# A SwiGLU layer's gate and up products with seven block products for eight over half of K

## The chip, the cores and the metric

One NeuronCore of one Trainium2 chip runs the whole program. The metric is device time in microseconds (us), the median over runs of the same program. The engines are TensorE (PE in the profile; PEld is its weight load), VectorE (DVE), ScalarE (ACT), GpSimd (POOL) and SyncE (SP, which here only issues transfers); 16 DMA engines move data.

## What is computed

A decoder layer over 256 tokens with a width of 2048, in float32: a token mixer of three attention branches, and then a dense SwiGLU layer, with a norm before each and at the end. The change lies in the second part (`w_gate` and `w_up` are 2048x5632, `w_down` 5632x2048):

```python
def rms_norm(x, g):
    y = x * lax.rsqrt(jnp.mean(x * x, axis=-1, keepdims=True) + RMS_EPS)
    return y * g

def swiglu(h, w_gate, w_up, w_down):
    return (jax.nn.silu(h @ w_gate) * (h @ w_up)) @ w_down

    ...
    h = rms_norm(x, norm_mix_g[l])
    x = x + hybrid_mixer(h, w_in[l], ...)
    h = rms_norm(x, norm_ffn_g[l])
    x = x + swiglu(h, w_ffn_gate[l], w_ffn_up[l], w_ffn_down[l])
    return rms_norm(x, final_norm_g)
```

## The kernel before

**Products in three parts.** TensorE multiplies in fp32r, a rounded float32. To keep float32's accuracy every operand is split into a high part (rounded to fp32r by a ScalarE copy) and a low part (the rest, subtracted on VectorE), and each product of a 128x128 stationary tile with a 128x512 moving tile is made three times: high x high, high x low, low x high (L714 to L716). The stationary tile is a piece of the transposed activations, the moving tile a piece of a weight matrix.

**Jobs, pieces and halves.** The program is one list of jobs (L194 to L199): 30 of `w_in`, 12 of `w_branch`, 4 of `w_out`, for each of the 11 column blocks j one of `w_fg` and one of `w_fu` (L552 to L554), 4 of `w_fd`. A job makes 512 output columns for both token tiles (t = 0, 1), in two banks of PSUM (`acc0`, `acc1`, from a pool of four). Its weights come in pieces of 512 rows (`raw`, 128x4x512, 1 MB), which SP loads three ahead into three buffers (`load`, L618). A piece is used in two halves. For each half `split` (L634) rounds 128x1024 on ScalarE (L655) and subtracts on VectorE (L656), three halves ahead of the products, into one of four buffers each; then come 12 products, 3 for each of two rows of K and two token tiles.

**Side work.** Transposes, attention and the like are generators in a queue; `advance(1)` takes one step of it before each half's products (L730), and a wanted operand that is not there is forced (`quad`, L156).

**The order.** The schedule is written out by hand: each engine runs its instructions in the order in which the program issues them, and waits by semaphores for the other engines' results and for buffers.

**Around the change.** The four `w_out` jobs end in `evac_out` (L491), which transposes x, times the norm's weight, into the quads `h2` (high and low parts, 512 rows of K each). The gate job's banks go through ScalarE's Silu with the norm's row factor into `sg` (L540); the up job's banks are multiplied by it on VectorE (L548). The product f is transposed by TensorE in two later side steps (L203, four transposes each) and split by ScalarE and VectorE (L212, L213) into 11 pairs of quads in the slot pool, which the down jobs read. The row factor of `up` is applied in the down jobs' evacuation.

```python
def evac_fu(j):
    def f(pss):
        s = sg.pop(j)
        for t in range(2):
            nc.vector.tensor_tensor(s[:, t], pss[t], s[:, t], OP.mult)
        side.append(to_quad(("f", j), s))
    return f
```

Of the kernel before, what the change touches and what calls it, by code (L numbers as in the profile page):

```python
# [23 lines left out]
F32 = mybir.dt.float32  # L24
F32R = mybir.dt.float32r
# [26 lines left out]
def trunk(ctx, tc, xT, x, gmix, gffn, w_in, b_gate, lq1, lk1, lq2, lk2, subln, w_branch, w_out,  # L52
          w_fg, w_fu, w_fd, gfin, out):
    nc = tc.nc
    cst = ctx.enter_context(tc.tile_pool(name="cst", bufs=1))
    raws = ctx.enter_context(tc.tile_pool(name="raws", bufs=RAW_BUFS))
    spl = ctx.enter_context(tc.tile_pool(name="spl", bufs=SPLIT_BUFS))
    hpool = ctx.enter_context(tc.tile_pool(name="hpool", bufs=4))
    slots = ctx.enter_context(tc.tile_pool(name="slots", bufs=SLOTS))

    small = ctx.enter_context(tc.tile_pool(name="small", bufs=4))
    accp = ctx.enter_context(tc.tile_pool(name="accp", bufs=4, space=bass.MemoryType.PSUM))
    side_ps = ctx.enter_context(tc.tile_pool(name="side_ps", bufs=2, space=bass.MemoryType.PSUM))
# [1 line left out]

    def slot(shape, name, dt=F32):
        return slots.tile(shape, dt, tag="slot", name=name)

    def sm(shape, name):
        return small.tile(shape, F32, name=name)  # L70
# [93 lines left out]

    def new_both():

        t = hpool.tile([P, 4, 2, S], F32R, tag="hq", name="hq")
        return t[:, :, 0], t[:, :, 1], t


    xq = {}
# [7 lines left out]
    def split_x(k):  # L179
        q = k // 4  # L180
        if q not in h_q:
            h_q[q] = new_both()
        h, l = h_q[q][:2]
# [302 lines left out]
    def row_rstd(dst, ssq):  # L486
        tot = sm([P, 2], "tot")
        nc.vector.tensor_reduce(tot, ssq, axis=AX.X, op=OP.add)
        rstd(dst, tot, float(D))

    def evac_out(c):  # L491
        def f(pss):
            xc = x2[c]
            for t in range(2):
                nc.vector.tensor_tensor(xc[:, t], pss[t], xc[:, t], OP.add)

            def go():
                yield
                both = new_both()
                h, l = both[:2]  # L500
                for kp in range(2):
                    ps = tps()
                    transposes(ps, [xc[:, t, (2 * kp + i) * P:(2 * kp + i + 1) * P]
                                    for i in range(2) for t in range(2)])
                    for i in range(2):
                        k = 2 * kp + i
                        gk = gf[:, 4 * c + k:4 * c + k + 1]
                        pk = ps[:, i * S:(i + 1) * S]
                        nc.scalar.activation(h[:, k], pk, AF.Copy, scale=gk)
                        nc.vector.scalar_tensor_tensor(l[:, k], pk, gk, h[:, k].bitcast(F32),  # L510
                                                       op0=OP.mult, op1=OP.subtract)
                    if kp == 1:
                        quads["h2", c] = both
                    yield
                row_sums(ssq2, c, xc)
                if c == 3:
# [12 lines left out]
        job([(w_out[c, kp], ("m", kp)) for kp in range(4)], evac_out(c))  # L529


    sg = {}

    def evac_fg(j):
        def f(pss):
            quad("rs2")
            s = slot([P, 2, 512], "sg")
            sg[j] = s
            for t in range(2):
                nc.scalar.activation(s[:, t], pss[t], AF.Silu, scale=rs2[:, t:t + 1])  # L540
        return f

    def evac_fu(j):

        def f(pss):
            s = sg.pop(j)
            for t in range(2):
                nc.vector.tensor_tensor(s[:, t], pss[t], s[:, t], OP.mult)  # L548
            side.append(to_quad(("f", j), s))
        return f  # L550

    for j in range(NCF):  # L552
        job([(w_fg[j, kp], ("h2", kp)) for kp in range(4)], evac_fg(j))
        job([(w_fu[j, kp], ("h2", kp)) for kp in range(4)], evac_fu(j))  # L554


    ssq3 = cst.tile([P, 2, 5], F32, name="ssq3")
# [1 line left out]
    gfs = {}  # L559

    def load_gfin():
        g = hpool.tile([P, 4, 512], F32, tag="hq", name="gfin")
# [47 lines left out]
    down_job = len(jobs)  # L610
    for c in range(4):
        job([(w_fd[c, kp], ("f", kp)) for kp in range(NCF)], evac_down(c))


    pieces = [(ji, pi) for ji, (ps, _) in enumerate(jobs) for pi in range(len(ps))]
    raw = {}

    def load(pidx):  # L618
        if pidx >= len(pieces):
            return  # L620
        ji, pi = pieces[pidx]
        ap = jobs[ji][0][pi][0]
        t = raws.tile([P, 4, 512], F32, tag="raw", name="raw")
        raw[pidx] = t
        if pidx < 4:
            for a, n in ((0, 1), (1, 1), (2, 2)) if pidx == 0 else ((0, 2), (2, 2)):
                load_xT(4 * pidx + a, n)
                nc.sync.dma_start(t[:, a:a + n], ap[:, a:a + n])  # L628
        else:
            nc.sync.dma_start(t, ap)  # L630

    parts = {}

    def split(hidx):  # L634
        if hidx >= 2 * len(pieces):
            return
        pidx, hf = divmod(hidx, 2)
        if 0 < hidx < 8:
            for i in range(2):
                split_x(2 * hidx + i)  # L640
        r = raw[pidx][:, 2 * hf:2 * hf + 2]
        if hidx < 2 * len(pieces) - LAST + SPLIT_BUFS:
            h = spl.tile([P, 2, 512], F32R, tag="wh", name="wh")
            l = spl.tile([P, 2, 512], F32R, tag="wl", name="wl")
        else:
            both = hpool.tile([P, 2, 2, 512], F32R, tag="hq", name="wboth")
            h, l = both[:, 0], both[:, 1]
        if hidx < 2:
            for i in range(2):
                if hidx == 0:  # L650
                    split_x(i)
                nc.scalar.activation(h[:, i], r[:, i], AF.Copy)
                nc.vector.tensor_tensor(l[:, i], r[:, i], h[:, i].bitcast(F32), OP.subtract)  # L653
        else:
            nc.scalar.activation(h, r, AF.Copy)  # L655
            nc.vector.tensor_tensor(l, r, h.bitcast(F32), OP.subtract)  # L656
        parts[hidx] = (h, l)
        if hf == 1:
            del raw[pidx]
            load(pidx + RAW_BUFS)  # L660

    def prepare():

# [31 lines left out]
        quads["rs"] = True  # L695
        yield

    for p in range(RAW_BUFS):
        load(p)
    for h in range(AHEAD):  # L700
        split(h)
    side.append(prepare())

    hidx = 0
    total = 2 * len(pieces)

    def products(acc, t, key, w, pi, hf, npieces):
        qh, ql = quad(key)[:2]
        wh, wl = w
        for i in range(2):  # L710
            k = 2 * hf + i
            a = qh[:, k, t * P:(t + 1) * P]
            b = ql[:, k, t * P:(t + 1) * P]
            nc.tensor.matmul(acc, a, wh[:, i], start=pi == 0 and k == 0, stop=False)  # L714
            nc.tensor.matmul(acc, a, wl[:, i], start=False, stop=False)  # L715
            nc.tensor.matmul(acc, b, wh[:, i], start=False, stop=pi == npieces - 1 and k == 3)  # L716

    for ji, (ps, evac) in enumerate(jobs):
        if ji in starts:
            load_bias(*starts[ji])  # L720
        if ji >= out_job and ji < out_job + 4:
            load_x(ji - out_job)
        if ji == down_job:
            load_gfin()
        acc = [accp.tile([P, 512], F32, tag="acc", name=f"acc{t}") for t in range(2)]
        late = []
        for pi in range(len(ps)):
            for hf in range(2):
                split(hidx + AHEAD)
                advance(1)  # L730
                args = (ps[pi][1], parts.pop(hidx), pi, hf, len(ps))
                products(acc[0], 0, *args)
                if hidx < total - LAST:
                    products(acc[1], 1, *args)
                else:
                    late.append(args)
                hidx += 1
        if late:
            finish(0, acc[0])
            for args in late:  # L740
                products(acc[1], 1, *args)
            finish(1, acc[1])
        else:
            evac(acc)
    assert not side


# [43 lines left out]
```

## Time and profile before

| | us |
|---|---|
| median of 3 runs (1688.86 to 1689.72) | 1689.5 |
| the profiled execution: its time | 1689.31 |
| the profiled execution: its span | 1687.6 |
| TensorE busy in the span | 1675.3 |
| VectorE busy | 928.4 |
| ScalarE busy | 757.0 |
| GpSimd busy | 28.4 |

The span runs from the first to the last instruction of the profiled execution. The busy time of an engine is the union of its instructions. Products of TensorE are pipelined, so the spacing of their starts, not the duration of one, says what a product costs. A line of the profile names the line of the kernel, the engine, and the tiles written and read; what ended an engine's idle time stands in square brackets or behind an arrow.

### The profile page before, as it was taken

How to read it: one execution, taken by the hardware profiler on the slowest of the kernel's cores; microseconds unless marked ns; L12 is line 12 of the kernel's file. 1: busy time of each engine (PE TensorE's matmuls, PEld its weight loads, DVE VectorE, ACT ScalarE, POOL GpSimd, SP SyncE). 2: the span in 40 equal slices, each digit the busy share in tenths (PEclk: the TensorE clock that was granted, in tenths of full speed). 3: DMA queues.
4: the chain of work that ended last, by engine and by line, in shares of the span. 5: the costliest groups of instructions: out<-in, count | busy, mean ns of one | idle time of the engine just before them, and what ended most of it. 6: DMA issues, size and time to landing. Idle time of an engine off the chain costs nothing.

```text
span 1687.6 us, 19009 instructions
## 1 busy us (share of the span) xinstructions
PE 1675.3 (99%) x7644; PEld 1380.5 (82%) x7644; DVE 928.4 (55%) x1074; ACT 757.0 (45%) x943; POOL 28.4 (2%) x43
## 2 busy tenths in 40 slices
PE   9999999999999999999999999999999999999997
PEld 6878788888888888888888888888888888888886
DVE  6676765656565656555565555444454445554454
ACT  6354544445444444444445544444444444444443
POOL 2100000000000000000000000000000000000000
PEclk9999999999999999999999999999999999999999
DMA  8545455455555655655655555555555556555553
GB/s 282 188 157 175 150 175 175 157 176 179 181 186 197 204 196 191 206 204 197 222 190 184 178 197 185 189 198 179 197 188 186 197 180 221 182 193 198 197 186 116
DMA packets 47321, 318.06 MB, mean 188 GB/s; under 512 B 5552, under 2 KB 5824, under 8 KB 10240
## 3 DMA queue, kind: packets, MB, share of 16 engines
q1 hardware_dynamic: 44640, 309.35, 52.7%
q0 software_dynamic: 1872, 6.43, 1.5%
q8 instruction: 60, 0.98, 0.2%
q10 hardware_dynamic: 720, 1.06, 0.2%
q14 instruction: 29, 0.24, 0.0%
HBM read 314.72 MB, written 2.10 MB: 188 GB/s over the span
## 4 chain that ended last, share of the span: by engine, by line
PE 99%; DMA 1%; ACT 0%; DVE 0%; SPq 0%; issue 0%; ACTq 0%
PE acc L714 32%; PE acc L716 31%; PE acc L715 31%; PE tps L203 2%; PE sps L242 1%; DMA raw<-w_in_t 1%; PE sps L255 0%; PE sps L256 0%; PE sps L254 0%; PE sps L293 0%; PE sps L294 0%; PE sps L295 0%; SPq L177 0%; ACT x L605 0%; SPq L628 0%; DVE wl L656 0%
## 5 line engine op out<-in xcount | busy, mean ns | idle before, releaser
L656 DVE TENSOR_TENSOR wl<-raw,wh 128x1024 fp32r<-128x1024 f32 x580 | 713.1, 1231 | 714.9 <-ACT wh L655 714.7
L655 ACT ACTIVATE wh<-raw 128x1024 fp32r<-128x1024 f32 x580 | 614.4, 1060 | 820.8 <-PE acc L716 798.1
L714 PE MATMUL acc<-wh,hq 128*128 128x512 f32 x1664 | 663.5, 399 | 0.1
L715 PE MATMUL acc<-wl,hq 128*128 128x512 f32 x1664 | 648.1, 390 | 1.7 <-DVE wl L653 1.0
L716 PE MATMUL acc<-wh,hq 128*128 128x512 f32 x1664 | 649.5, 390 | 0.0
L716 PEld LDWEIGHTS acc<-wh,hq 128*128 128x128 f32 x1664 | 312.3, 188 | 67.4
L715 PEld LDWEIGHTS acc<-wl,hq 128*128 128x128 f32 x1664 | 313.1, 188 | 65.0 <-DVE wl L653 2.2
L714 PEld LDWEIGHTS acc<-wh,hq 128*128 128x128 f32 x1664 | 312.7, 188 | 64.5 <-issue 2.7
L714 PE MATMUL acc<-wh,th 128*128 128x512 f32 x472 | 184.6, 391 | 0.0
L716 PE MATMUL acc<-wh,tl 128*128 128x512 f32 x472 | 183.8, 389 | 0.0
L715 PE MATMUL acc<-wl,th 128*128 128x512 f32 x472 | 183.6, 389 | 0.0
L716 PEld LDWEIGHTS acc<-wh,tl 128*128 128x128 f32 x472 | 88.6, 188 | 18.5
L715 PEld LDWEIGHTS acc<-wl,th 128*128 128x128 f32 x472 | 88.6, 188 | 18.1
L714 PEld LDWEIGHTS acc<-wh,th 128*128 128x128 f32 x472 | 88.6, 188 | 18.2
L714 PE MATMUL acc<-wh,oh 128*128 128x512 f32 x192 | 74.7, 389 | 0.0
L715 PE MATMUL acc<-wl,oh 128*128 128x512 f32 x192 | 74.7, 389 | 0.0
L716 PE MATMUL acc<-wh,ol 128*128 128x512 f32 x192 | 74.7, 389 | 0.0
L716 PEld LDWEIGHTS acc<-wh,ol 128*128 128x128 f32 x192 | 36.0, 188 | 7.5
L715 PEld LDWEIGHTS acc<-wl,oh 128*128 128x128 f32 x192 | 36.0, 188 | 7.5
L714 PEld LDWEIGHTS acc<-wh,oh 128*128 128x128 f32 x192 | 36.0, 188 | 7.5
L266 ACT ACTIVATE sc<-sc,mx 128x128 f32<-128x128 f32 (+1 forms) x32 | 14.3, 448 | 20.2 <-DVE mx L264 19.3
L213 DVE TENSOR_TENSOR tl<-tps,th 128x512 fp32r<-128x512 f32 x30 | 20.5, 684 | 0.0
(161 smaller groups left out, 602.9 us busy)
## 6 DMA issues: line engine op xcount, KB each, us to landing
raw<-w_in_t SPq DMA_DIRECT2D x116, 1024.0 KB, 4.8
raw<-w_fg_t SPq DMA_DIRECT2D x44, 1024.0 KB, 4.8
raw<-w_fu_t SPq DMA_DIRECT2D x44, 1024.0 KB, 4.9
raw<-w_fd_t SPq DMA_DIRECT2D x44, 1024.0 KB, 4.8
raw<-w_branch_t SPq DMA_DIRECT2D x24, 1024.0 KB, 4.8
raw<-w_out_t SPq DMA_DIRECT2D x16, 1024.0 KB, 4.8
raw<-w_in_t SPq DMA_DIRECT2D x7, 512.0 KB, 8.7
bias<-b_gate_r POOLq DMA_DIRECT2D x12, 256.0 KB, 4.2
```

What stands on the lines that cost most here:

```text
L203: nc.tensor.transpose(dst[:, i * P:(i + 1) * P], s, ident)
L213: nc.vector.tensor_tensor(l, ps, h.bitcast(F32), OP.subtract)
L242: nc.tensor.matmul(ps[:, a:b], qt[lo:hi, h, t * P:(t + 1) * P], kt[lo:hi, h, 0:b - a], start=True, stop=True)
L266: nc.scalar.activation(sc[:, a:b], sc[:, a:b], AF.Exp, bias=mx[:, t:t + 1], accum_out=sums[:, t:t + 1])
L655: nc.scalar.activation(h, r, AF.Copy)
L656: nc.vector.tensor_tensor(l, r, h.bitcast(F32), OP.subtract)
L714: nc.tensor.matmul(acc, a, wh[:, i], start=pi == 0 and k == 0, stop=False)
L715: nc.tensor.matmul(acc, a, wl[:, i], start=False, stop=False)
L716: nc.tensor.matmul(acc, b, wh[:, i], start=False, stop=pi == npieces - 1 and k == 3)
```

## The change

**Block products.** For a block j let B[k, n] be the piece of `w_fu` (n = 0) or `w_fg` (n = 1) with the rows k. Over the pieces k = 0 and 1 the two token tiles, the two pieces of K and the two matrices make a 2x2x2 block product. It is now made of seven products (Winograd's form of Strassen's) with operands that are sums: seven combinations of h2, made once (`combine`), and sums of raw weight pieces, made in place by a VectorE add before the splitting (`add`). The pieces 2 and 3 are multiplied as before.

**Units.** The list of jobs becomes a list of units with a `prep` and an `emit`. In a gate and up block there are 11: seven product units (`m_unit`, one bank, 12 products each), of which the third, fifth, seventh and tenth begin with an add of 128x2048, and four plain units (`p_unit`, two banks, 24 products each). They come in the order M, M, M+add, P, M+add, P, M+add, M, P, M+add, P. Each splits a whole piece, 128x2048, in one ScalarE and one VectorE instruction (`whole`), and takes two buffers. At most three units are held (`PARTS`, counted in buffers): before unit u is emitted, u+2 is prepared. Six raw pieces may be loaded (`RAWS`). Mixer and down units stay halves, three ahead.

**Banks.** The block's four banks hold the partial results; copies of three intermediate states of bank b6 and b8 (`keep`) go to SBUF by ScalarE, and six VectorE operations of 512 columns add and multiply them (`keep`, `last`). The Silu stands behind the seventh unit.

**f through DRAM.** f is transposed as before, copied by ScalarE alone, stored to DRAM by POOL's queue (`f_out`), loaded again two pieces before it is wanted and split in the first down job (`f_load`, `f_split`).

**Pools.** The buffers for raw pieces, weight parts and the quads h become one pool of 12 tiles of 8 KB per partition (`bigs`); the slot pool has 25 instead of 27.

The core of the diff (with the units' loops cut):

```diff
-RAW_BUFS = 3
-SPLIT_BUFS = 4
-AHEAD = 3
-SLOTS = 27
+BIGS = 12
+SLOTS = 25
+RAWS = {"mix": 3, "ffn": 6, "down": 3}
+PARTS = {"mix": 4, "ffn": 6, "down": 4}
...
+    def combine(key, h1, h2):
+        a = {(t, q): h[:, :, t * P:(t + 1) * P] for t in range(2) for q, h in enumerate((h1, h2))}
+        t12 = slot([P, 2, 4, P], "s12")
+        t34 = slot([P, 2, 4, P], "s34")
+        s1, s2, s3, s4 = t12[:, 0], t12[:, 1], t34[:, 0], t34[:, 1]
+        nc.vector.tensor_tensor(s1, a[1, 0], a[1, 1], OP.subtract)
+        nc.vector.tensor_tensor(s2, s1, a[0, 0], OP.subtract)
+        nc.vector.tensor_tensor(s3, a[0, 0], a[1, 0], OP.subtract)
+        nc.vector.tensor_tensor(s4, a[0, 1], s2, OP.add)
+        yield
+        ops = []
+        for v in (a[0, 0], a[0, 1], s4, a[1, 1], s1, s2, s3):
+            p = slot([P, 2, 4, P], "sp", F32R)
+            nc.scalar.activation(p[:, 0], v, AF.Copy)
+            nc.vector.tensor_tensor(p[:, 1], v, p[:, 0].bitcast(F32), OP.subtract)
+            ops.append((p[:, 0], p[:, 1]))
+            yield
+        quads[key] = ops
+        yield
...
+    def f_out(j, f):
+        yield
+        ft = slot([P, 4, S], "ft")
+        for t in range(2):
+            ps = tps()
+            transposes(ps, [f[:, t, i * P:(i + 1) * P] for i in range(4)])
+            nc.scalar.activation(ft[:, :, t * P:(t + 1) * P], ps.rearrange("p (a b) -> p a b", a=4), AF.Copy)
+            if t == 1:
+                nc.gpsimd.dma_start(f_t[j], ft)
+            yield
+    f_in = {}
+    def f_load(q):
+        if q < NCF:
+            f_in[q] = slot([P, 4, S], "fin")
+            nc.gpsimd.dma_start(f_in[q], f_t[q])
+    def f_split(q):
+        h, l = new_both() if q < 4 else new_quad("f")
+        src = f_in.pop(q)
+        nc.scalar.activation(h, src, AF.Copy)
+        nc.vector.tensor_tensor(l, src, h.bitcast(F32), OP.subtract)
+        quads["f", q] = (h, l)
+    def ffn_job(j):
+        B = {(k, n): (j, k, n) for k in range(4) for n in range(2)}
+        B11, B12, B21, B22 = B[0, 0], B[0, 1], B[1, 0], B[1, 1]
+        aps = {(j, k, n): (w_fu, w_fg)[n][j, k] for k in range(4) for n in range(2)}
+        for key in (B22, B11, B12, B[2, 1], B[3, 1], B21, B[2, 0], B[3, 0]):
+            want(key, aps[key], "ffn")
+        bank = {}
+        v = {}
+        def add(dst, src):
+            nc.vector.tensor_tensor(raw[dst], raw[dst], raw[src], OP.add)
+        def m_unit(op, key, name, adds=(), drop=(), after=None):
+            def prep():
+                for d, s in adds:
+                    add(d, s)
+                w = whole(raw[key])
+                release(*drop)
+                return w
+            def emit(w):
+                first = name not in bank
+                if first:
+                    bank[name] = accp.tile([P, 512], F32, tag="acc", name="acc")
+                sh, sl = quad(("s", 0))[op]
+                three(bank[name], sh, sl, w, first, True, True)
+                if after:
+                    after()
+            units.append((2, "ffn", prep, emit))
...
+        def keep(name, b):
+            def f():
+                if name == "m1":
+                    v["m"] = slot([P, 2, 512], "m")
+                    v["u"] = slot([P, 2, 512], "u")
+                v[name] = v["m" if name[0] == "m" else "u"][:, int(name in ("m5", "u3"))]
+                nc.scalar.activation(v[name], bank[b], AF.Copy)
+                if name == "u2":
+                    nc.vector.tensor_tensor(v["m5"], v["m5"], v["u2"], OP.subtract)
+                if name == "u3":
+                    quad("rs2")
+                    s = v["s"] = slot([P, 2, 512], "sg")
+                    nc.vector.tensor_tensor(s[:, 0], bank["b5"], v["m5"], OP.add)
+                    nc.vector.tensor_tensor(s[:, 1], bank["b8"], v["u3"], OP.subtract)
+                    for t in range(2):
+                        nc.scalar.activation(s[:, t], s[:, t], AF.Silu, scale=rs2[:, t:t + 1])
+            return f
+        def last():
+            s = v["s"]
+            nc.vector.tensor_tensor(s[:, 1], bank["b6"], s[:, 1], OP.mult)
+            nc.vector.tensor_tensor(v["m1"], bank["b1"], v["m1"], OP.add)
+            nc.vector.tensor_tensor(s[:, 0], v["m1"], s[:, 0], OP.mult)
+            side.append(f_out(j, s))
+        m_unit(2, B22, "b5")
+        m_unit(0, B11, "b6", after=keep("m1", "b6"))
+        m_unit(4, B11, "b8", adds=[(B11, B12)], after=keep("m5", "b8"))
+        p_unit(2, 1)
+        m_unit(5, B11, "b6", adds=[(B11, B22)], after=keep("u2", "b6"))
+        p_unit(3, 1)
+        m_unit(6, B12, "b6", adds=[(B12, B22)], drop=[B12, B22], after=keep("u3", "b6"))
+        m_unit(1, B21, "b1")
+        p_unit(2, 0, after=(lambda: (f_load(0), f_load(1))) if j == NCF - 1 else None)
+        m_unit(3, B11, "b6", adds=[(B11, B21)], drop=[B11, B21])
+        p_unit(3, 0, after=last)
...
+    def pump():
+        while loaded[0] < len(wanted) and len(raw) < RAWS[wanted[loaded[0]][2]]:
+            key, ap, _ = wanted[loaded[0]]
+            n = loaded[0]
+            t = raw[key] = big([P, 4, 512], "raw")
...
+    def release(*keys):
+        for k in keys:
+            del raw[k]
+        pump()
...
+    def whole(r):
+        h = big([P, 4, 512], "wh", F32R)
+        l = big([P, 4, 512], "wl", F32R)
+        nc.scalar.activation(h, r, AF.Copy)
+        nc.vector.tensor_tensor(l, r, h.bitcast(F32), OP.subtract)
+        return h, l
...
+    def prepare_units(n):
+        nonlocal at, held
+        while at < len(units) and at < n:
+            need, stage, prep, _ = units[at]
+            if held + need > PARTS[stage]:
+                break
+            ready.append(prep())
+            held += need
+            at += 1
+    prepare_units(3)
     side.append(prepare())
...
+    for u, (need, stage, _, emit) in enumerate(units):
+        prepare_units(u + 4 if stage == "mix" else len(units))
+        advance(1)
+        emit(ready.popleft())
+        held -= need
```

## Rows read from the trace of the kernel before

**Rows 1.** The page's first part: busy time, share and instructions of each engine.

```profile
PE 1675.3 (99%) x7644; PEld 1380.5 (82%) x7644; DVE 928.4 (55%) x1074; ACT 757.0 (45%) x943; POOL 28.4 (2%) x43
```

**Rows 2.** The page's chain that ended last, by engine.

```profile
PE 99%; DMA 1%; ACT 0%; DVE 0%; SPq 0%; issue 0%; ACTq 0%
```

**Rows 3.** Windows: stretch, length, busy us per engine (PE to POOL), granted clock, DMA share, GB/s.

```profile
5.00:10.00 5.00, 4.04 (x13) 2.20 (x12) 3.66 (x5) 2.77 (x6) 3.91 (x10) 1.00 1.01 280
...
800.00:955.00 155.00, 155.00 (x705) 128.31 (x704) 88.24 (x92) 71.04 (x86) 1.43 (x2) 1.00 0.57 197
...
970.00:1422.00 452.00, 452.00 (x2034) 374.24 (x2033) 223.84 (x203) 196.86 (x207) 0.00 (x0) 1.00 0.55 189
...
1680.00:1688.00 8.00, 0.00 (x0) 0.00 (x0) 2.66 (x10) 1.44 (x2) 0.00 (x0) 0.68 0.35 131
```

**Rows 4.** Tile sg, and ScalarE's timeline: the Silu of the gate product.

```profile
L540 ACT ACTIVATE sg<-acc,rs x22: 682/690/691, 971.4 to 1416.5; 128x512 f32<-128x512 f32 x22
...
1016.22 0.69 ACT L540 ACTIVATE sg<-acc,rs 128x512 f32<-128x512 f32 x1 [0.67 <-PE acc L716]
```

**Rows 5.** Timeline of TensorE, two products that stand fifteen steps apart.

```profile
1046.22 0.39 PE L714 MATMUL acc<-wh,hq 128*128 128x512 f32 x1
...
1049.62 0.39 PE L714 MATMUL acc<-wh,hq 128*128 128x512 f32 x1
```

**Rows 6.** Waits: who waited for whom, us in total, times, longest.

```profile
ACT wh L655 <- PE acc L716: 798.1, 488, 2.2
...
DVE wl L656 <- ACT wh L655: 714.7, 538, 2.4
```

**Rows 7.** Groups of instructions by line and shape: busy us, mean ns, idle before.

```profile
L656 DVE TENSOR_TENSOR wl<-raw,wh 128x1024 fp32r<-128x1024 f32 x580 | 713.1, 1231 | 714.9 <-ACT wh L655 714.7
...
L655 ACT ACTIVATE wh<-raw 128x1024 fp32r<-128x1024 f32 x580 | 614.4, 1060 | 820.8 <-PE acc L716 798.1 <-issue 12.5 <-ACT sig L434 7.7
...
L212 ACT ACTIVATE th<-tps 128x512 fp32r<-128x512 f32 x30 | 17.4, 581 | 0.0
...
L548 DVE TENSOR_TENSOR sg<-acc,sg 128x512 f32<-128x512 f32 x22 | 14.1, 682 | 0.0
...
L458 DVE TENSOR_TENSOR sig<-sig,sig 128x1024 f32<-128x1024 f32 x8 | 9.8, 1225 | 0.3
...
L401 ACT ACTIVATE k<-acc 128x512 f32<-128x512 f32 x12 | 7.2, 599 | 7.4 <-PE acc L716 7.4
...
L582 DVE TENSOR_TENSOR x<-x,gfin 128x512 f32<-128x512 f32 x6 | 4.0, 690 | 0.3
...
L652 ACT ACTIVATE wh<-raw 128x512 fp32r<-128x512 f32 x4 | 2.4, 627 | 3.4 <-DMA raw<-w_in_t 3.4
```

**Rows 8.** Timeline of VectorE and ScalarE in the gate and up stage.

```profile
1036.36 1.23 DVE L656 TENSOR_TENSOR wl<-raw,wh 128x1024 fp32r<-128x1024 f32 x1 [1.49 <-ACT wh L655]
...
1037.50 1.28 DVE L548 TENSOR_TENSOR sg<-acc,sg 128x512 f32<-128x512 f32 x2
...
1040.71 1.06 ACT L655 ACTIVATE wh<-raw 128x1024 fp32r<-128x1024 f32 x1 [1.66 <-PE acc L716]
...
1041.80 1.23 DVE L656 TENSOR_TENSOR wl<-raw,wh 128x1024 fp32r<-128x1024 f32 x1 [1.50 <-ACT wh L655]
```

**Rows 9.** DMA issues: KB each and median us to landing.

```profile
raw<-w_fg_t SPq DMA_DIRECT2D x44, 1024.0 KB, 4.8
...
x<-x_nat POOLq DMA_DIRECT2D x4, 512.0 KB, 4.8
```

More of the change, by code (lines that the diff above doesn't have):

```diff
@@ new lines, in trunk, with p_unit, prep, emit @@
+    f_in = {}
[35 more added lines that the diff above has]
+            units.append((2, "ffn", prep, emit))
+        def p_unit(k, n, after=None):
+            def prep():
+                w = whole(raw[B[k, n]])
+                release(B[k, n])
+                return w
+            def emit(w):
+                qh, ql = quad(("h2", k))
+                for t, name in enumerate((("b1", "b6"), ("b5", "b8"))[n]):
+                    first = name not in bank
+                    if first:
+                        bank[name] = accp.tile([P, 512], F32, tag="acc", name="acc")
+                    three(bank[name], qh[:, :, t * P:(t + 1) * P], ql[:, :, t * P:(t + 1) * P], w, first, True,
+                          True)
+                if after:
+                    after()
+            units.append((2, "ffn", prep, emit))
+        def keep(name, b):
[32 more added lines that the diff above has]
+        p_unit(3, 0, after=last)
@@ L632, in trunk @@
[L632 to L660, printed above, removed]
+    units = []
@@ new lines, in plain_job, with unit, prep, emit @@
+    def plain_job(ji, stage, pieces, evac, before=None, lastjob=False):
+        acc = []
+        late = []
+        def unit(pi, hf):
+            key = (ji, pi)
+            def prep():
+                if ji == 0 and (pi or hf):
+                    for i in range(2):
+                        split_x(4 * pi + 2 * hf + i)
+                if stage == "down" and ji == down0 and hf == 0:
+                    f_load(pi + 2)
+                    f_split(pi)
+                w = half(raw[key][:, 2 * hf:2 * hf + 2], (1 + hf) if ji == 0 and pi == 0 else 0)
+                if hf:
+                    release(key)
+                return w
+            def emit(w):
+                first = pi == 0 and hf == 0
+                final = pi == len(pieces) - 1 and hf == 1
+                if first:
+                    if before:
+                        before()
+                    acc.extend(accp.tile([P, 512], F32, tag="acc", name=f"acc{t}") for t in range(2))
+                def part(t, w=w):
+                    qh, ql = quad(pieces[pi][1])
+                    k = slice(2 * hf, 2 * hf + 2)
+                    three(acc[t], qh[:, k, t * P:(t + 1) * P], ql[:, k, t * P:(t + 1) * P], w, first, final)
+                part(0)
+                if lastjob and 2 * (len(pieces) - pi) - hf <= LAST:
+                    late.append(part)
+                else:
+                    part(1)
+                if final:
+                    if lastjob:
+                        finish(0, acc[0])
+                        for p in late:
+                            p(1)
+                        finish(1, acc[1])
+                    else:
+                        evac(acc)
+            units.append((1, stage, prep, emit))
+        for pi, (ap, _) in enumerate(pieces):
+            want((ji, pi), ap, stage)
+            for hf in range(2):
+                unit(pi, hf)
@@ new lines, in trunk @@
+    for ji, (ps, evac) in enumerate(jobs):
+        before = None
+        if ji in starts:
+            before = lambda a=starts[ji]: load_bias(*a)
+        elif ji >= out_job:
+            before = lambda c=ji - out_job: load_x(c)
+        plain_job(ji, "mix", ps, evac, before)
+    for j in range(NCF):
+        ffn_job(j)
+    down0 = len(jobs)
+    for c in range(4):
+        plain_job(down0 + c, "down", [(w_fd[c, kp], ("f", kp)) for kp in range(NCF)],
+                  evac_down(c), None if c else load_gfin, c == 3)
@@ L696, in prepare @@
         yield
[L698 to L701, printed above, removed]
-    side.append(prepare())
[L704 to L744, printed above, removed]
+    pump()
+    ready = deque()
+    held = 0
+    at = 0
+    def prepare_units(n):
[8 more added lines that the diff above has]
+    prepare_units(3)
+    side.append(prepare())
+    for u, (need, stage, _, emit) in enumerate(units):
[3 more added lines that the diff above has]
+        held -= need
     assert not side
```

98 lines of the change are left out of this document (51 added, 47 removed).

## The prediction

> **What bounds the kernel now.** I read the page's engine shares first: TensorE is busy 99% of the 1687.6 us span, VectorE 55%, ScalarE 45% [rows 1]. The chain that ended last is TensorE for 99% of its length [rows 2]. So in every stage a cycle taken from TensorE is time, until another engine takes its place; how near the others are has to be read by stage. In the gate and up stage (970 to 1422 us) TensorE is busy all 452.0 us, VectorE 223.8 and ScalarE 196.9, at a granted clock of 1.00 [rows 3]. One column block j (its gate and its up job) takes (1416.5 - 1016.22) / 9 = 44.48 us, from the Silu of the second block to that of the eleventh [rows 4]. Products follow each other at 3.40 us / 15 = 0.2267 us [rows 5]; 192 of them are 43.53 us, and the other 0.95 us are the eight transposes of f. VectorE and ScalarE are followers: ScalarE's rounding waits 798.1 us for TensorE to free a buffer, VectorE's subtraction 714.7 us for that rounding [rows 6]. The second row matters below: VectorE stands still while ScalarE rounds.
>
> **What the change takes away.** Per block the half of K in pieces 0 and 1 costs 7 x 12 = 84 products instead of 96, the other half 96 as before: 180 x 0.2267 + 0.95 = 41.76 us of TensorE. Over 11 blocks that is 132 products less, 29.9 us. VectorE also loses the two low parts of f's transposes (0.68 us each) and gets them back as eleven 1024-column splits in the first down job.
>
> **What it adds on VectorE, per block.** Each of the eleven units makes one rounding (ScalarE) and one subtraction (VectorE) over 128x2048, and four units first add two raw pieces in place. No row has 2048 columns. An f32 add of 1024 columns takes 1225 ns, the subtraction 1231, an SBUF operation of 512 columns 690 [rows 7]: 1.05 ns a column, so 2.30 us for 2048. The bounds are two operations of 1024 columns, 2 x 1.231 = 2.46 us when nothing is shared and 2 x 1.14 = 2.28 at their closest spacing [rows 8]; I take 2.30, on the line through the rows. In the same way ScalarE's rounding goes from 627 and 1060 ns to 1.93 us [rows 7]. The six 512-column operations that join the banks take 0.68 us each like the product of gate and up now [rows 7]. Two operations with no wait between them overlap: two of 682 ns stand in 1.28 us, and the first of them starts 1.14 us after the start of one of 1.23 us, so 0.09 us is saved at each start [rows 8].
> So VectorE needs 15 x 2.21 + 6 x 0.59 = 36.7 us per block, under TensorE's 41.76. By the sum of its work the change would win.
>
> **Where the wait is.** The instructions of one unit are issued in one piece: add (VectorE), round (ScalarE), subtract (VectorE). Nothing of the next unit stands between add and subtract in VectorE's queue, and [rows 6] show that VectorE lets nothing pass. In a unit with an add, VectorE waits 0.03 us of hand-over each way (a rounding that ends at 1041.77 releases a subtraction at 1041.80 [rows 8]), 1.93 us of rounding and loses the 0.09 us of overlap: 2.08 us, four times, 8.3 us. Behind the waiting subtraction stand the bank sums and the next unit's add, and TensorE, whose second product of the unit needs the low part. In units without an add the rounding runs beside the subtraction before it. 36.7 + 8.3 = 45.0 us: already over the 44.48 us of now.
> Then come waits for TensorE. A unit holds its two buffers until its products are done, and three units are held; so the rounding of unit u+3 starts when TensorE ends unit u. I laid the three queues out in program order with these durations (products 2.72 us in a product unit, 5.44 in a plain one; a result can be read 0.20 us after the last product). Three waits remain per block: 0.65 us where the block's closing sum needs its last plain unit (VectorE comes to it 0.45 us before TensorE is done), 0.63 where the sixth unit's rounding stands behind two copies out of PSUM (0.58 and 0.60 us [rows 7]), 0.41 where the next block's second unit waits for a buffer. 45.0 + 1.7 = 46.7 us. TensorE, with 41.8 us of work, stands still 4.9 us per block, at most 1.7 us at once. The bounds: without these waits 45.0; with wide operations of 2.46 us the layout gives 48.5; with no overlap and hand-overs of 0.1 us also 48.5.
>
> A page of the Trainium skill prices these operations lower: "VectorE: DVE Perf Modes", section on the TRN2 errata, gives 58 + columns cycles at 0.96 GHz. By it a 2048-column operation takes an estimated 2.19 us and the block some 1.6 us less, 45.1. The trace speaks against it: 1024 columns would be 1.13 us, and the row has 1.231 [rows 7].
>
> **The other edits, at nothing, with their cover.** The combinations of h2: 11 VectorE operations of 512 columns (7.5 us) and seven copies, once, in the last two w_out jobs, where VectorE is busy 88.2 of 155 us [rows 3]; uncovered 7.5 us. f through DRAM: a 512 KB store and load each, like x's 512 KB, which lands in 4.8 us [rows 9]; block 0 is stored ten blocks before the first down job reads it, block 10 some seven pieces of 5.44 us before its load is issued. They stand in POOL's queue, with only the final gain's load behind them. In the first down job VectorE has three 1.23 us operations per 24 products of 5.44 us: 3.7 us, covered; uncovered 11 x 1.2 = 13. The weights: eight loads of 1 MB per 46.7 us, 4.8 us each [rows 9], with up to six pieces waiting. SP's queue holds them as now and its waits on a freed piece hide behind that lead. The four banks: between the products that fill a bank and the next that write it lie at least 2.7 us of other products, and the copy takes 0.60; if a copy comes late, TensorE waits for that lateness, and the 4.9 us of idle time take it in. Pool and slots: 12 tiles are exactly what six pieces and three units fill, so no load waits for another. At the two ends of the stage I take 0, within 0 to 3 us.
>
> **Sum.** The profiled execution took 1689.31 us (span 1687.6, the rest lies outside it); the median of the runs is 1689.5. 1689.3 + 11 x (46.7 - 44.48) = 1689.3 + 24.4 = 1714 us.
>
> **Rivals.**
> TensorE stays the bound, the other side: if VectorE is given other work during the four roundings, its block is 36.7 us and some waits, TensorE's 41.8 decides, and the time is 1689.3 - 11 x 2.7 = 1660 us. It starts to win from the point where 2.2 us of the 10 us of waits are gone. For it speaks VectorE's sum; against it the order in which a unit is issued and the 538 waits for the rounding now. Chance 0.13.
> Saving and wait cancel: a block of 44.3 to 44.8 us, 1687 to 1693, if the wide operations are some 5% shorter than the line of the rows. Chance 0.05.
> The dear chain: no overlap, longer hand-overs and some of the covers gone, over 48.5 us per block, 1738 to 1755. For it speaks that a stalled TensorE ends later than laid out, which delays the buffers; against it the overlap that the rows have [rows 8]. Chance 0.07.
> The clock falls: TensorE's stalls would now recur in every block. At the lower level (1.2 GHz) products take 0.453 us, a block 82.5, the time 1689 + 11 x 38 = 2107. At the start TensorE stood still about 1 us of 5 at a granted clock of 1.00; it fell only in the end, with no products [rows 3]. The Trainium skill's page "TensorE: Matmul & The Clock Gate", section on why this matters for kernels, warns of idle gaps between bursts; these rows show no fall with gaps of this size. Chance 0.02.
>
> **The numbers.** The forecast has 0.73: 45.0 to 48.5 us per block, 1695 to 1734, and with the open ends of 3 us either way 1692 to 1738. The range is that; it leaves out the fast rival, most of the dear one and the clock, about 0.2. A measurement of this kernel tells 0.2% (3.4 us) from no change. Faster 0.13, same 0.05, slower 0.82.
>
> **What would show it.** Right: Silu of successive blocks some 46.7 us apart; 44 adds and 121 subtractions of about 2.30 us; VectorE busy about 38.6 us per block in the lengths shown; each subtraction behind an add idle some 2 us for the rounding; TensorE waiting for VectorE's low parts, about 54 us in total, where it waits for nothing now; the chain running through VectorE and ScalarE in this stage alone; mixing and down stages as long as now. Wrong: blocks of 42 us with TensorE's idle time near zero; wide operations well under 2.2 us; a granted clock under 1; TensorE idle in the first down job; waits that name a DMA.

## The result, and the profile after

The changed kernel takes 1730.8 us (median of 4, 1729.85 to 1731.68) against 1689.3: 1.0246 times as long, 95% interval [1.0228, 1.0263]. The forecast was 1714 in 1692 to 1738: the side and the mechanism came true, the loss is 41.5 us where 24.4 were forecast. The span of the profiled execution went from 1687.6 to 1729.9 us, by 42.3.

The page's engine shares and the chain that ended last, by engine (as in [rows 1, 2]):

```profile
PE 1675.6 (97%) x7512; PEld 1367.3 (79%) x7512; DVE 1113.9 (64%) x1099; ACT 829.2 (48%) x950; POOL 40.0 (2%) x65
...
PE 74%; DVE 16%; ACT 7%; issue 2%; DMA 1%; SPq 0%; ACTq 0%; DVEq 0%
```

TensorE has its 132 products less, yet its busy time is as before: busy time counts slower products in full and, as the products overlap, hides short gaps. What changed is the chain: a quarter of it is no longer TensorE. To see where, take windows: from the first product of the first block to that block's join, a later block from join to join, most of the first down job, and the later ones (columns as in [rows 3]).

```profile
948.00:985.90 37.90, 30.83 (x129) 24.57 (x128) 27.66 (x30) 20.21 (x24) 0.00 (x0) 0.91 0.34 114
1082.58:1130.28 47.70, 44.44 (x190) 35.60 (x189) 37.35 (x23) 25.00 (x19) 0.53 (x1) 0.96 0.50 188
...
1500.00:1560.00 60.00, 60.00 (x267) 49.67 (x266) 37.58 (x37) 29.26 (x31) 0.00 (x0) 1.00 0.60 210
1560.00:1720.00 160.00, 160.00 (x708) 132.49 (x707) 77.19 (x78) 63.65 (x70) 0.00 (x0) 1.00 0.50 178
```

TensorE is busy throughout the down jobs, with f's splits in the first of them (VectorE 37.6 of 60 us, against 77.2 of 160). The loss is in the gate and up stage. There the first operation that reads a block's banks (L659, just ahead of the Silu of [rows 4]) marks the blocks:

```profile
L659 DVE TENSOR_TENSOR sg<-acc,m x11: 678/684/685, 985.9 to 1464.4; 128x512 f32<-128x512 f32 x11
...
1034.86 0.68 DVE L659 TENSOR_TENSOR sg<-acc,m 128x512 f32<-128x512 f32 x1
```

From the second to the eleventh a block takes (1464.4 - 1034.86) / 9 = 47.73 us, where it took 44.48 and 46.7 were forecast. That is 11 x 3.25 = 35.8 us. The first block needs 37.9 us from its first product (947.99) to its join, a later one 31.75 (1098.53 to 1130.28): another 6.2. Together 41.9 of the 42.3; 0.4 us is left for the stage's end and the other stages.

The groups that the forecast had to size, and who waited for whom (as in [rows 7] and [rows 6]):

```profile
L782 DVE TENSOR_TENSOR wl<-raw,wh 128x2048 fp32r<-128x2048 f32 x121 | 273.5, 2289 | 107.7 <-ACT wh L781 101.2 <-issue 5.3 <-PE acc L775 1.3
L781 ACT ACTIVATE wh<-raw 128x2048 fp32r<-128x2048 f32 x121 | 229.4, 1913 | 216.1 <-DVE raw L609 193.3 <-PE acc L775 11.9 <-DVE wl L782 5.6
...
L609 DVE TENSOR_TENSOR raw<-raw 128x2048 f32<-128x2048 f32 x44 | 100.5, 2283 | 0.0
```

```profile
ACT wh L781 <- DVE raw L609: 193.3, 44, 7.8
DVE wl L782 <- ACT wh L781: 101.2, 58, 2.4
...
PE acc L774 <- DVE wl L782: 31.9, 22, 1.8
PE acc L773 <- ACT m L653: 9.1, 11, 5.0
```

A rounding waits for the add (44 times), a subtraction for the rounding, TensorE for the subtraction. One whole block of VectorE shows it (start, us, engine, line; in brackets the idle time before and what ended it):

```profile
1082.58 0.68 DVE L659 TENSOR_TENSOR sg<-acc,m 128x512 f32<-128x512 f32 x1
1083.18 0.68 DVE L660 TENSOR_TENSOR sg<-acc,u 128x512 f32<-128x512 f32 x1
1083.78 2.28 DVE L609 TENSOR_TENSOR raw<-raw 128x2048 f32<-128x2048 f32 x1
1088.11 4.49 DVE L782 TENSOR_TENSOR wl<-raw,wh 128x2048 fp32r<-128x2048 f32 x2 [2.04 <-ACT wh L781]
1093.12 4.49 DVE L782 TENSOR_TENSOR wl<-raw,wh 128x2048 fp32r<-128x2048 f32 x2 [0.52 <-issue]
1098.73 0.69 DVE L668 TENSOR_TENSOR sg<-acc,sg 128x512 f32<-128x512 f32 x1 [1.12 <-PE acc L775]
1099.34 0.68 DVE L669 TENSOR_TENSOR m<-acc,m 128x512 f32<-128x512 f32 x1
1100.06 0.69 DVE L670 TENSOR_TENSOR sg<-m,sg 128x512 f32<-128x512 f32 x1
1100.66 2.29 DVE L609 TENSOR_TENSOR raw<-raw 128x2048 f32<-128x2048 f32 x1
1104.99 4.49 DVE L782 TENSOR_TENSOR wl<-raw,wh 128x2048 fp32r<-128x2048 f32 x2 [2.04 <-ACT wh L781]
1109.40 2.29 DVE L609 TENSOR_TENSOR raw<-raw 128x2048 f32<-128x2048 f32 x1
1113.73 2.29 DVE L782 TENSOR_TENSOR wl<-raw,wh 128x2048 fp32r<-128x2048 f32 x1 [2.04 <-ACT wh L781]
1116.50 2.29 DVE L782 TENSOR_TENSOR wl<-raw,wh 128x2048 fp32r<-128x2048 f32 x1 [0.48 <-ACT wh L781]
1118.71 2.28 DVE L609 TENSOR_TENSOR raw<-raw 128x2048 f32<-128x2048 f32 x1
1123.06 2.29 DVE L782 TENSOR_TENSOR wl<-raw,wh 128x2048 fp32r<-128x2048 f32 x1 [2.07 <-ACT wh L781]
1125.27 0.69 DVE L655 TENSOR_TENSOR m<-m,u 128x512 f32<-128x512 f32 x1
1125.87 4.49 DVE L782 TENSOR_TENSOR wl<-raw,wh 128x2048 fp32r<-128x2048 f32 x2
1130.28 0.69 DVE L659 TENSOR_TENSOR sg<-acc,m 128x512 f32<-128x512 f32 x1
```

Behind each of the four adds VectorE stands still for 2.04 to 2.07 us; elsewhere it waits 0.52, 1.12 and 0.48.

### The profile page after: what moved, and what is told of

It reads as the page before. It is cut to its first block, busy times and chain, and to the rows that moved or that the text cites. A ratio compares the mean times of both kernels' runs of the same rounds, so it can differ in the third digit from the quotient of the medians.

```text
span 1729.9 us, 18605 instructions
## 1 busy us (share of the span) xinstructions
PE 1675.6 (97%) x7512; PEld 1367.3 (79%) x7512; DVE 1113.9 (64%) x1099; ACT 829.2 (48%) x950; POOL 40.0 (2%) x65
## 4 chain that ended last, share of the span: by engine, by line
PE 74%; DVE 16%; ACT 7%; issue 2%; DMA 1%; SPq 0%; ACTq 0%; DVEq 0%
PE acc L774 23%; PE acc L775 23%; PE acc L773 23%; DVE wl L782 8%; ACT wh L781 6%; DVE raw L609 6%; PE tps L206 2%; PE sps L245 1%; DMA raw<-w_in_t 1%; DVE sg L670 0%; DVE sg L668 0%; DVE sg L659 0%; DVE sg L660 0%; DVE m L669 0%; ACT m L653 0%
## 5 line engine op out<-in xcount | busy, mean ns | idle before, releaser
L792 DVE TENSOR_TENSOR wboth<-raw,wboth 128x1024 fp32r<-128x1024 f32 (+1 forms) x410 | 499.8, 1230 | 298.6 <-ACT wboth L791 298.2
L791 ACT ACTIVATE wboth<-raw 128x1024 fp32r<-128x1024 f32 (+1 forms) x410 | 426.9, 1053 | 405.4 <-PE acc L775 307.7
L773 PE MATMUL acc<-wboth,hq 128*128 128x512 f32 x1088 | 437.0, 402 | 0.5 <-ACT wboth L791 0.4
L774 PE MATMUL acc<-wboth,hq 128*128 128x512 f32 x1088 | 424.0, 390 | 1.6 <-DVE wboth L792 1.6
L775 PE MATMUL acc<-wboth,hq 128*128 128x512 f32 x1088 | 425.1, 391 | 0.0
L782 DVE TENSOR_TENSOR wl<-raw,wh 128x2048 fp32r<-128x2048 f32 x121 | 273.5, 2289 | 107.7 <-ACT wh L781 101.2
L781 ACT ACTIVATE wh<-raw 128x2048 fp32r<-128x2048 f32 x121 | 229.4, 1913 | 216.1 <-DVE raw L609 193.3
L775 PEld LDWEIGHTS acc<-wboth,hq 128*128 128x128 f32 x1088 | 204.2, 188 | 44.3
L773 PEld LDWEIGHTS acc<-wboth,hq 128*128 128x128 f32 x1088 | 204.4, 188 | 43.7 <-issue 2.7
L774 PEld LDWEIGHTS acc<-wboth,hq 128*128 128x128 f32 x1088 | 204.7, 188 | 42.9 <-DVE wboth L792 2.9
L774 PE MATMUL acc<-wl,sp 128*128 128x512 f32 x308 | 127.9, 415 | 31.9 <-DVE wl L782 31.9
L773 PE MATMUL acc<-wh,h2h 128*128 128x512 f32 x352 | 141.0, 400 | 9.1 <-ACT m L653 9.1
L774 PE MATMUL acc<-wl,h2h 128*128 128x512 f32 x352 | 139.0, 395 | 0.0
L773 PE MATMUL acc<-wh,sp 128*128 128x512 f32 x308 | 127.2, 413 | 0.0
L775 PE MATMUL acc<-wh,sp 128*128 128x512 f32 x308 | 126.2, 410 | 0.0
L774 PE MATMUL acc<-wboth,fh 128*128 128x512 f32 x224 | 87.1, 389 | 0.0
L773 PE MATMUL acc<-wboth,fh 128*128 128x512 f32 x224 | 87.1, 389 | 0.0
```

Of the source, the lines that this page charges most:

```text
L773: nc.tensor.matmul(acc, ah[:, k], wh[:, k], start=start and k == 0, stop=False, skip_group_check=skip)
L774: nc.tensor.matmul(acc, ah[:, k], wl[:, k], start=False, stop=False, skip_group_check=skip)
L775: nc.tensor.matmul(acc, al[:, k], wh[:, k], start=False, stop=stop and k == n - 1, skip_group_check=skip)
L791: nc.scalar.activation(h[:, sl], r[:, sl], AF.Copy)
L792: nc.vector.tensor_tensor(l[:, sl], r[:, sl], h[:, sl].bitcast(F32), OP.subtract)
```

## The experiments

Three theories were set against each other. A: the wait between an add and its subtraction, with the rounding in between, sets the pace. B: VectorE's added work does. C: TensorE does, which runs some products at the lower clock after its stalls and waits for a bank.

**Adds one unit earlier** (`e1_early`). `whole` issues the next unit's adds between its rounding and its subtraction; the first two units change places, so that no piece is changed before it is used.

```diff
-    def whole(r):
+    def whole(r, between=None):
...
         nc.scalar.activation(h, r, AF.Copy)
+        if between:
+            between()
         nc.vector.tensor_tensor(l, r, h.bitcast(F32), OP.subtract)
...
-            ready.append(prep())
+            ready.append(prep(units[at + 1][4] if at + 1 < len(units) else None))
```

> The four adds are issued one unit earlier, between the rounding and the subtraction of the unit before (units one and two change places so that the sums stay right); the work of every engine is as in the changed kernel. Theory A (VectorE's wait for ScalarE's rounding between an add and its subtraction sets the pace): the wait is filled, TensorE is the bound again, a block takes 41.8 to 42.5 us instead of 47.7 and the run 1660 to 1670 us, the first block's extra included. Theory B (VectorE's added work itself, or a slower VectorE, is the cost): a block stays over 46 us, over 1710 us. Theory C (TensorE's lower clock after its stalls and its late banks are the cost): they come from the stalls, so partly gone, 1690 to 1715 us.

1670.75 us, 0.9891 [0.9876, 0.9906] of the kernel before: 60 us less than the changed kernel with the same work. A block takes 42.58 us ((1404.4 - 978.6) / 10); block and time lie just over the top of what A gave (42.5 and 1670) and far from B and C. B has fallen. TensorE's waits for these low parts shrink from 31.9 to 1.4 us in all, and a new one shows, for the closing sums:

```profile
PE tps L206 <- DVE sg L672: 6.0, 10, 0.6
...
PE acc L776 <- DVE wl L786: 1.4, 2, 0.7
```

**The same work without the dependence** (`e2_otherdst`). The sum goes into the other piece, so the rounding reads a piece that the add leaves alone, and the products use it unsummed.

```diff
-            nc.vector.tensor_tensor(raw[dst], raw[dst], raw[src], OP.add)
+            nc.vector.tensor_tensor(raw[src], raw[dst], raw[src], OP.add)
```

> Each add writes its sum over its second operand instead of the piece that is rounded next, so that the rounding no longer needs the add; the sums of weights are therefore not used, the output leaves them out. The work and its order are those of the changed kernel, only the dependence is gone. Theory A: 41.8 to 43 us per block, 1660 to 1675 us. Theory B: as the changed kernel, 1725 us or more. Theory C: 1690 to 1715 us.

1664.1 us (one run), a block (1395.7 - 979.0) / 10 = 41.67 us: the 41.76 of TensorE's work alone that the prediction had worked out. With the order left as it is and every wide operation still made, taking the dependence away is worth 67 us. Shown: the wait, not the work, costs the time.

**Products that nobody reads in TensorE's stalls** (`e4_fill`), 7 in the third and 4 in the tenth unit.

```diff
+            if k == 0 and fill:
+                junk = sps()
+                for _ in range(fill):
+                    nc.tensor.matmul(junk, ah[:, k], wh[:, k], start=True, stop=True)
...
-                three(bank[name], sh, sl, w, first, True, True)
+                three(bank[name], sh, sl, w, first, True, True, {4: 7, 3: 4}.get(op, 0))
```

> In the third and the tenth unit of a block TensorE makes 7 and 4 products that nobody reads, between its first product and the one that waits for the low part: about the length of its two stalls. Theory A: the lower clock (eight products of the third unit at 0.427 us instead of 0.227) hides in VectorE's wait, the granted clock rises to 1.00 in the blocks, and the time stays within 4 us of 1731. Theory C: the fall costs its full 1.6 us per block or more, the time goes down by 15 to 25 us. Theory B says nothing of it.

1731.9 us, 1.0252 [1.0236, 1.0267] of the kernel before: as without them. The clock did rise, from 0.97 in the same two windows of the changed kernel to these (columns as in [rows 3], the granted clock third from the end):

```profile
1040.00:1140.00 100.00, 95.36 (x412) 76.27 (x411) 77.81 (x44) 52.23 (x40) 1.09 (x2) 0.98 0.50 189
1140.00:1440.00 300.00, 286.02 (x1259) 229.68 (x1258) 234.31 (x133) 155.48 (x117) 3.20 (x6) 1.00 0.48 180
```

The added products lengthen nothing: behind them TensorE still waits for the low part, 20 times and 4.6 us in all. What it gains it now waits for bank b8 (23.4 us instead of 9.1 in total). The clock's half of C has fallen for the steady blocks: there it costs nothing that a run can show.

**Low parts last** (`e5_lowlast`).

```diff
+        if again:
+            for i, (x, y) in enumerate(((ah, wh), (al, wh), (ah, wl))):
+                for k in range(n):
+                    nc.tensor.matmul(acc, x[:, k], y[:, k], start=start and i == 0 and k == 0,
+                                     stop=stop and i == 2 and k == n - 1, skip_group_check=skip)
+            return
```

> In the gate and up units all products with the rounded weights come first and the four with the low part last, so TensorE needs the low part eight products (1.8 us) later and is done earlier after it. Theory A: the four waits for the rounding (8.5 us per block) stay, the ones for TensorE (about 2.4 us) mostly go; a block takes 45.5 to 46.5 us, the run 1706 to 1718 us. Theory B: 1725 us or more. Theory C: no stall, full clock, 1665 to 1690 us.

A miss: 1730.1 us, 1.0244 [1.0227, 1.0261], nothing gained. Taken alone that is what B gave; the two runs above rule B out. TensorE's wait for low parts nearly went (2.1 us in total), but another took its place, for the copy of a bank (40.1 us in total), here in one block of that run (ScalarE's timeline, then TensorE's):

```profile
1109.09 1.91 ACT L787 ACTIVATE wh<-raw 128x2048 fp32r<-128x2048 f32 x1 [3.99 <-DVE raw L609]
1110.90 0.58 ACT L575 ACTIVATE ft<-tps 128x512 f32<-128x512 f32 x1
1111.38 0.59 ACT L653 ACTIVATE m<-acc 128x512 f32<-128x512 f32 x1
...
1112.02 1.20 PE L775 MATMUL acc<-wh,h2h 128*128 128x512 f32 x4 [3.36 <-ACT m L653]
```

The fourth unit's second token tile writes bank b8, which ScalarE must have copied before. The copy stands in ScalarE's queue behind the fifth unit's rounding, and that waits for the fifth unit's add: the add holds TensorE up a second way.

**The bank's copy one unit later, with and without this order** (`e8_lowlast_latecopy`, `e9_latecopy`).

```diff
-        m_unit(4, B11, "b8", adds=[(B11, B12)], after=keep("m5", "b8"))
-        p_unit(2, 1)
+        m_unit(4, B11, "b8", adds=[(B11, B12)])
+        p_unit(2, 1, after=keep("m5", "b8"))
```

> As e5_lowlast, but the copy of bank b8 comes one unit later, after other products have been added to the bank, so the output has other sums and TensorE does not wait for the copy in the fourth unit. If that copy, behind a rounding that waits for an add, took the gain of e5_lowlast: a block of 45.5 to 46.5 us, 1706 to 1718 us. If the waits for the rounding alone hold the pace at 47.5 us whatever TensorE does: 1726 to 1732 us.

> The changed kernel with the same late copy of bank b8 alone (other sums in the output). The bank's wait is 0.3 to 0.5 us per block there and lies in TensorE's idle time: Theory A 1724 to 1732 us, no more than 5 us off; if the bank's wait counts in full, 1725 at most by 0.5 x 11.

With the order of `e5_lowlast` 1706.1 us (here and below one run each), a block (1440.5 - 985.4) / 10 = 45.51: what A had given for `e5_lowlast`. VectorE's only waits there are the four behind the adds, 42.4 us in five blocks, 8.5 in one. So 45.5 us is the chain of adds, roundings and subtractions by itself. Alone the late copy gives 1725.5 us, 5.3 less: just over A's bound, and close to what the bank's wait in full would give. VectorE's waits tell why: in five blocks they fall from 43.4 to 41.2 us behind roundings and from 25 to 20 in number, 0.44 us less per block and 4.8 in eleven. The wait of 0.48 us at the sixth unit is gone, since its rounding no longer has the copy ahead of it. The bank's own wait lay in TensorE's idle time: without it TensorE waits longer for low parts, 39.7 us instead of 31.9 in total.

**Eight plain products in the new structure** (`e3_plain8`): units, the one pool, the trip through DRAM and 25 slots stay; `combine`, the sums and the bank copies go.

```diff
+        for k in range(4):
+            p_unit(k, 1, after=gate if k == 3 else None)
+        for k in range(4):
+            p_unit(k, 0, after=up if k == 3 else (lambda: (f_load(0), f_load(1))) if k == 2 and j == NCF - 1 else None)
...
-        m_unit(2, B22, "b5")
-        m_unit(0, B11, "b6", after=keep("m1", "b6"))
...
-        p_unit(3, 0, after=last)
```

> The units, the one pool, six raw pieces, f through DRAM and the smaller slot pool stay, but all of K is multiplied by plain units, eight block products: no adds, no combinations of h2, no copies of banks. Theory A (the whole loss lies in the block products' adds and their waits): as the kernel before, 1686 to 1695 us, a block 44.3 to 44.8 us. Theory D (part of the loss lies in the DRAM trip, the pools or the whole pieces): over 1700 us.

1690.9 us, 1.0007 [0.9997, 1.0017]. None of the edits that stay costs anything that can be measured; of `combine` this run says nothing.

**What e1_early left** (`e7_early_yield`, `e10_early_yield_low`, `e6_early_lowlast`). In `f_out` one more `yield` puts the transposes a step later; the other edit is that of `e5_lowlast`.

> The adds one unit earlier as in e1_early, and the transposes of f one side step later, since there TensorE waited 0.6 us per block for the closing sums, which stand behind one more wide add now. Theory A: a block comes from 42.6 down to 41.7 to 42.0 us, the run from 1670.8 to 1660 to 1665 us. If the transposes' wait is only moved to the next product, it stays at 1669 to 1672 us.

1672.0 us, 0.9895 [0.9881, 0.9910]: the wait only moved, from the transposes (6.0 us in all) to the fourth unit's low part (7.7 us).

> The adds one unit earlier, the transposes one side step later, and the products with the low part last in a unit: in e7_early_yield TensorE waited 0.7 us per block for the low part of the fourth unit, in e1_early 0.6 us for the closing sums. Theory A (only waits of TensorE on VectorE's queue are left above its 41.7 us of work): a block 41.6 to 41.9 us, 1660 to 1665 us. If the wait only moves again: 1669 to 1673 us.

1665.8 us, 0.9862 [0.9845, 0.9878]; a block (1399.4 - 979.0) / 10 = 42.04 us, a little over what A gave.

> As e10_early_yield_low without the later transposes. If the closing sums are what is left, TensorE waits 0.4 to 0.6 us per block for them and the run takes 1665 to 1670 us; if the low part was it in both, 1660 to 1664 us.

1663.5 us (one run), the second of its two cases: with the low parts last, TensorE waits for the closing sums once in the stage, 1.5 us. The same kernel in more runs:

> The kernel of e6_early_lowlast, timed in rounds: Theory A 1662 to 1666 us, 0.984 to 0.986 of the kernel before, TensorE without a wait in the steady blocks.

1663.6 us (median of 4, 1663.37 to 1663.93), 0.9844 [0.9828, 0.9861] of the kernel before and 67 us under the changed kernel. It beats both. TensorE in its blocks (windows as above):

```profile
1040.00:1140.00 100.00, 100.00 (x451) 82.44 (x450) 89.79 (x51) 60.50 (x47) 1.62 (x3) 1.00 0.58 214
1140.00:1380.00 240.00, 240.00 (x1080) 197.68 (x1079) 214.01 (x122) 144.23 (x110) 2.66 (x5) 1.00 0.57 213
```

A block takes (1397.0 - 979.1) / 10 = 41.79 us. Of the saving of 29.9 us all but 4 is in it, most of those outside the steady blocks (11 x (44.48 - 41.79) = 29.6).

## Why the prediction was right, and what it had too small

The measured loss is some 17 us over the forecast one. Two terms make it up, both too small: the block (11.3 us in all) and the beginning of the stage (6.2). The result stays in the range because the block was given 45.0 to 48.5 us; the 6.2 us lie outside what the ends were given.

**The place and the sign: right.** Nearly all of the loss lies in the gate and up stage, VectorE's queue stands still behind every add for ScalarE's rounding, and with that dependence gone (`e2_otherdst`) or filled (`e1_early`) the time falls below that of the kernel before.

**The durations: right.** 2.283 us for the add and 2.289 for the subtraction where 2.30 was taken, 1.913 for the rounding where 1.93 was. The row of the Trainium skill's page "VectorE: DVE Perf Modes", in its errata section, by which the prediction had an estimated 2.19, is below what this trace shows. The same section of the Trainium skill gives 2.291 us for an f32 addition of 2048 columns, and with that the trace agrees: the prediction had read only the lower of its two figures.

**TensorE's own work: right.** 41.76 us per block were forecast; `e2_otherdst` runs at 41.67.

**The covers: right.** The DRAM trip, the pools and the slots were costed at nothing, and `e3_plain8` finds 1.0007. The combinations too: up to the first product of the stage TensorE is never idle in this stretch (columns as in [rows 3]), and that product starts at 947.99 us, in the kernel before at 948.36.

```profile
800.00:948.00 148.00, 148.00 (x670) 122.52 (x669) 85.70 (x87) 67.34 (x82) 2.14 (x3) 1.00 0.60 213
```

f's store and load took their time beside other work, the load longer than x's 4.8 us of [rows 9]:

```profile
f_t<-ft POOLq DMA_DIRECT2D x11, 512.0 KB, 2.9
fin<-f_t POOLq DMA_DIRECT2D x11, 512.0 KB, 8.0
```

**The block: 1.0 us too small (47.73 against 46.7, 11 us in all).** The step is "Three waits remain per block", 1.7 us. The largest share is the closing sum. It costs 1.12 us of idle time and 0.09 of lost overlap, 1.21 where 0.65 was forecast: 0.56. VectorE reaches it 0.92 us before TensorE goes on to the next unit (1097.61 against 1098.53), where 0.45 was laid out. The first of the three closing operations reads b6, the bank that the last unit fills last, so all three wait; whether the layout had let it go ahead, the prediction does not say. The four waits behind adds cost 2.05 + 0.09 where 2.08 was forecast, 0.2 in all: an add that ends at 1086.06 releases a rounding at 1086.16, a hand-over of 0.10 us, not 0.03. The two small ones (0.52 and 0.48, each with 0.09 of lost overlap, where 0.41 and 0.63 were forecast) add 0.1. With VectorE's waits for TensorE out of the way, as in `e8_lowlast_latecopy`, the block is 45.5 us; the prediction's lower bound was 45.0.

**The ends of the stage: 6.2 us, taken as 0 within 0 to 3.** The step is "At the two ends of the stage I take 0". The end is free; the beginning isn't. VectorE sets the pace of the first block too (it waits 8.7 us for roundings and never for TensorE), and its queue also holds the last side work of the w_out jobs, h2's splits (L542) and the norm's row factor (from L491 up to L655):

```profile
964.88 0.48 DVE L542 SCALAR_TENSOR_TENSOR h2l<-tps,gf,h2h 128x256 fp32r<-128x256 f32 x1
...
968.18 2.29 DVE L782 TENSOR_TENSOR wl<-raw,wh 128x2048 fp32r<-128x2048 f32 x1 [1.80 <-ACT wh L781]
970.39 0.48 DVE L542 SCALAR_TENSOR_TENSOR h2l<-tps,gf,h2h 128x256 fp32r<-128x256 f32 x1
...
971.82 2.28 DVE L609 TENSOR_TENSOR raw<-raw 128x2048 f32<-128x2048 f32 x1
...
978.35 0.16 DVE L491 TENSOR_REDUCE tot<-ssq 128x2 f32<-128x8 f32 x1
...
980.59 0.68 DVE L655 TENSOR_TENSOR m<-m,u 128x512 f32<-128x512 f32 x1
...
985.93 0.68 DVE L659 TENSOR_TENSOR sg<-acc,m 128x512 f32<-128x512 f32 x1
```

The splits take 1.50 and 1.43 us with the waits in them, the row factor 2.24, and a copy just before the join 0.33: 5.5 us that a later block does not have. The waits for roundings are 2.0 us longer than in the same stretch of a later block, and VectorE comes to its first add 1.3 us sooner after the block's first product: 5.5 + 2.0 - 1.3 = 6.2. This is read from the trace; no run took the side work away.

TensorE's longest stall, in the same block, is not the cost:

```profile
966.41 0.79 PE L773 MATMUL acc<-wh,h2h 128*128 128x512 f32 x1 [5.00 <-ACT m L653]
```

In `e9_latecopy` this wait for bank b8 is gone, and from the first product (948.28) to the join (985.75) the block still takes 37.5 us, against 37.9.

**The banks.** The prediction had a late copy vanish in TensorE's idle time. In the changed kernel that is right (`e9_latecopy`: what it gains is a wait of VectorE), but the wait is there in every block, and as soon as TensorE's other stall goes it takes its place, as `e5_lowlast` found.

**The rival of the lower clock** (0.02) was priced as a whole stage at 1.2 GHz. That did not come; short falls did (below), and `e4_fill` shows that they are not what costs the time. So one of the prediction's signs of being wrong, a granted clock under 1, showed without it being wrong.

**TensorE's waits for low parts: "about 54 us in total" came to 31.9.** TensorE does lose more than that, 47.73 - 41.76 = 6.0 us per block. But only about 3.0 of it are these waits; about 1.6 are eight products at 0.427 us instead of 0.227, 0.3 the wait for bank b8, and the rest lies around the stalls.

## What to carry to other kernels

When an engine's total work fits, look for an in-order queue that hands work to another engine and takes it back: A to B to A costs B's whole time on A, once per round trip, unless something else of A's is issued in between (here 2.05 us of VectorE for a rounding of 1.91, 44 times). Taking out the dependence while keeping the work is the quickest proof that a wait and not the work is the cost. And after one wait of an engine is gone, ask which of its others has been lying beneath it: here the low part, the copied bank and the closing sums each came up in turn.

## What the runs showed of the hardware

The rows of the prediction showed no fall of TensorE's clock in the middle of the work. Here it fell: in the nine blocks from the third on it went to its lower level after this (TensorE's timeline, where a product's start-to-start time is what counts):

```profile
1104.47 0.60 PE L206 MATMUL tps<-ident,sg 128*128 128x128 f32 x4
1105.01 0.49 PE L773 MATMUL acc<-wh,sp 128*128 128x512 f32 x1
1107.34 0.50 PE L774 MATMUL acc<-wl,sp 128*128 128x512 f32 x1 [1.83 <-DVE wl L782]
...
1108.65 0.63 PE L775 MATMUL acc<-wh,sp 128*128 128x512 f32 x1
1109.07 0.63 PE L773 MATMUL acc<-wh,sp 128*128 128x512 f32 x1
```

Four transposes, one product and 1.83 us of standing still, then, 0.9 us after work went on, eight products 0.427 us apart instead of 0.227: the lower of the two levels, 1.2 GHz, with a granted clock of 0.96 over the block. The other stall of that block, 1.15 us with products on both sides, was followed by products 0.23 us apart. With products put into both stalls (`e4_fill`) the granted clock is 0.98 to 1.00.

The same stall does not always bring the fall. In the second block of the changed kernel 1.83 us of standing still, up to 1010.71, were followed by products 0.23 us apart, and the slower ones came behind a wait of 1.87 us for bank b8, up to 1018.09. In `e9_latecopy` the transposes, the one product and the stall of 1.82 to 1.83 us stand in ten blocks, and slower products follow in four of them. What decides it, and whether the transposes have a part in it, these runs do not show.
